# A decoder trunk on one core: nine instead of six blocks of each MLP's second product in the seven-product form

## The chip, the cores and the metric

The kernel runs on one core of a Trainium2 chip. The metric is the device time of one execution in microseconds; the time of a kernel is the median of several executions. Before the change this is 611.49 us (three executions, 611.18 to 611.83).

Of the core's engines five matter: TensorE (matrix products; PE in the profile, its weight loads PEld), VectorE (DVE), ScalarE (ACT), GpSimd (POOL) and SyncE (SP), whose queue issues the transfers of the weights.

## The reference

The program is a two-layer decoder trunk on 256 tokens of width 1024, in float32:

```python
def sqrelu_mlp(x, w1, w2):
    h = jax.nn.relu(x @ w1)
    return (h * h) @ w2

for layer in range(DEPTH):                       # DEPTH = 2
    hn = rms_norm(h, norm_gain[layer, 0])
    h = h + (stick_breaking_attention(hn, ...) if layer == 0 else nsa_attention(hn, ...))
    h = h + sqrelu_mlp(rms_norm(h, norm_gain[layer, 1]), mlp_w1[layer], mlp_w2[layer])
return rms_norm(h, final_norm)
```

w1 is 1024 x 4096 and w2 4096 x 1024. The change touches the two MLPs only.

## The kernel before

**Products of split numbers.** Each float32 operand a is split into a rounded part (h, cast to fp32r by ScalarE) and the rest (l = a - h, by VectorE). A product a b is then three matmuls: ah bh, ah bl, al bh (`mm3`, L209 to L211). In the first product of the MLP two of these go into one matmul 512 columns wide (L214, `wide`).

**Weights** come as tiles of 128 x 2048, one transfer each, in the order of use. `fetch` issues a transfer when one of three raw buffers is free; `split` (L121) makes the h and l tiles (wh, wl, three buffers each, shared by w1 and w2) in two steps of 1024 columns: a cast on ScalarE (L155), a subtraction on VectorE (L158). `step` calls it as work goes on, up to three tiles ahead.

**A block of the MLP.** The 4096 hidden columns are cut into 16 blocks c of 256. Tile wa[c] holds w1's columns of block c, wb[c] the two row blocks of w2 (each 128 x 1024). For each block the first product is made in two halves f = 0, 1 of 16 matmuls (`products`, L375) into a bank pu. `evac` (L384) copies the bank on ScalarE (mr) and adds its two parts on VectorE (mu, L390). After both halves `hidden` (L392) applies relu and the norm's scale (L396), squares (ScalarE, L398), and splits into hh and hl (L410, L411), with the sums that the second product needs (hx, L402 to L408).

**The second product** of a block is a 2 x 2 product: two hidden halves by two token tiles, against two row blocks of w2 and two column halves of 512. It takes eight products of 128 x 512 (`plain`), or, for blocks in FEWER, seven by Winograd's form (`fewer`), whose operands are sums of the hidden tiles and sums of w2's quarters. Each entry of the tables is (bank, hidden tile, which weights: 0 for w2's own split and 1 for the sums, first column). The first four entries run behind the next block's second half (part 0), the others in the middle of the block after that, between its two halves (part 1). The extra banks of the seven-product form are put together once by `fold`, behind block 12.

**The sums of w2.** For a block in FEWER `split` takes a branch (L135 to L149). It makes four sums of 512 columns (tx, 2048 wide, one buffer; L141, L143, L144), splits them into tp (one buffer, 2048 columns of h and of l), and splits the three quarters of w2 itself that are needed (1536 columns).

**The order.** TensorE's order is that of the code here (it is kept). A scheduler with its own costs places the instructions of the other engines, each of which runs its list in order.

Of the kernel before, what the change touches and what calls it, by code (L numbers as in the profile page):

```python
# [7 lines left out]
F32 = mybir.dt.float32  # L8
F32R = mybir.dt.float32r
# [5 lines left out]
P = 128  # L15
D = 1024
# [12 lines left out]
NEG = -1e30  # L29
GELU_C = 2.0 * 0.7978845608028654  # L30

FEWER = (2, 4, 6, 8, 10, 12)

C_ID, C_CA, C_CAP, C_ANY, C_COS, C_SIN, C_BLK, C_PW, C_END = (
    0, 128, 256, 640, 642, 674, 706, 710, 711)
# [29 lines left out]
def hybrid_kernel(ctx, tc, x, xca, xcb, eye, gcols, gfin, wqk, wva, wvb, wo0, wkv, wq, wg, rot, wo1, w1, w2, cw1, cw2, cpos, gate_b, cmask, consts, out):  # L65
    nc = tc.nc
# [8 lines left out]
    def f32(a):  # L75
        return a.bitcast(F32)
# [4 lines left out]
    def pair(shape, name):  # L81

        return cp.tile([P, 2, *shape], F32R, tag="x", name=name, bufs=2)

    def bank(name, dt=F32):
        return ps.tile([P, 512], dt, tag="a", name=name, bufs=4)
# [11 lines left out]
    made, raws = [], {}  # L98
# [3 lines left out]
    mixed = {}  # L102
# [18 lines left out]
    def split(pin=False):  # L121

        j, c = at
        src, n, plain = stream[j]
        if plain:

            made.append([wp.tile([P, n], F32, tag=f"w{a}", name="wc", bufs=3) for a in "hl"])
            for a in range(2):
                nc.sync.dma_start(made[j][a], src[a])
            at[:] = (j + 1, 0)  # L130
            return
        if c == 0:
            made.append((wp.tile([P, n], F32R, tag="wh", name="wh", bufs=3),
                         wp.tile([P, n], F32R, tag="wl", name="wl", bufs=3)))
        if j in mixed:  # L135
            h, lo = made[j]
            four = raws[j].rearrange("p (a q) -> p a q", q=512)
            tx, th, tl = mixed[j]()
            t4 = tx.rearrange("p (a q) -> p a q", q=512)
            if c == 0:  # L140
                nc.vector.tensor_sub(t4[:, 0:2, :], four[:, 1::2, :], four[:, 0:2, :])  # L141
            else:
                nc.vector.tensor_sub(t4[:, 2, :], four[:, 3, :], t4[:, 0, :])  # L143
                nc.vector.tensor_sub(t4[:, 3, :], four[:, 2, :], t4[:, 2, :])  # L144
            for dh, dl, src, r in ((h, lo, raws[j], slice(c, c + (1024 if c else 512))), (th, tl, tx, slice(c, c + 1024))):
                nc.scalar.copy(dh[:, r], src[:, r])  # L146
                nc.vector.tensor_sub(dl[:, r], src[:, r], f32(dh[:, r]))  # L147
            at[:] = (j, 1024) if c == 0 else (j + 1, 0)
            if c:  # L149
                fetch()  # L150
            return
        m = n // 4 if j < 2 else n // 2
        r = slice(c, c + m)
        h, lo = made[j]
        ins = nc.scalar.copy(h[:, r], raws[j][:, r])  # L155
        if pin:
            tc.keep_in_program_order(ins)
        nc.vector.tensor_sub(lo[:, r], raws[j][:, r], f32(h[:, r]))  # L158
        at[:] = (j, c + m) if c + m < n else (j + 1, 0)
        if c + m == n and j != NV - 1:  # L160
            fetch()
# [160 lines left out]
    def mlp(layer, gi, xt, mid, ap):  # L322

        wa, wb = i_m[layer]
        tp = pair([2048], "tp")
        tx = []

        def sums():
            if not tx:
                tx.append(ap.tile([P, 2048], F32, name="tx", bufs=1))  # L330
            return tx[0], tp[:, 0], tp[:, 1]

        for c in FEWER:
            mixed[wb[c]] = sums
        bank_of = {}
        last_few = FEWER[-1]

        plain = ((2, 1, 0, 0), (2, 3, 0, 1024), (4, 0, 0, 0), (4, 2, 0, 1024),
                 (5, 0, 0, 512), (5, 2, 0, 1536), (3, 4, 0, 512), (3, 5, 0, 1536))
        fewer = ((1, 1, 0, 0), (2, 3, 0, 1024), (3, 7, 0, 1536), (4, 2, 1, 1536),  # L340
                 (5, 4, 1, 0), (6, 5, 1, 1024), (7, 6, 1, 512))

        def product(m, a, kind, o, hT, c, q=slice(0, 512), o_bank=None, first=False):
            w = W(wb[c])
            if kind:
                w = sums()[1:]
            if o_bank is None:
                first = m not in bank_of
                if first:
                    bank_of[m] = bank(f"acc{m}") if 2 <= m <= 5 else zs[{1: 1, 6: 3, 7: 2}[m]]  # L350
                o_bank = bank_of[m]
            mm3(o_bank[:, q], (hT[0][:, a, :], hT[1][:, a, :]), cut(w, o + q.start, o + q.stop), first,
                c == NFC - 1 or c == last_few and m in (1, 6, 7))

        def second(c, hT, part):
            ps_ = fewer if c in FEWER else plain
            for i, e in enumerate(ps_[:4] if part == 0 else ps_[4:]):
# [26 lines left out]
        def evac(c, f, pu):  # L384
            if c not in parts:
                parts[c] = ap.tile([P, 2, 512], F32, name="mr", bufs=1), ap.tile([P, 512], F32, name="mu")
            r, u = parts[c]
            with tc.high_priority(offset=300):
                nc.scalar.copy(r[:, f, :], pu)  # L389
            nc.vector.tensor_add(u[:, f * 256:(f + 1) * 256], r[:, f, 0:256], r[:, f, 256:512])  # L390

        def hidden(c):  # L392
            r, u = parts.pop(c)
            few = c in FEWER
            uv = u.rearrange("p (f q) -> p f q", f=2)
# [60 lines left out]
        for c in range(3, NFC):  # L456
# [22 lines left out]
            h = hidden(c)  # L479
# [744 lines left out]
```

## Time and profile before

| | before |
|---|---|
| median of the runs | 611.49 us |
| span of the profiled execution | 609.3 us |
| TensorE busy | 598.4 us (98%) |
| VectorE busy | 503.4 us (83%) |
| ScalarE busy | 397.8 us (65%) |
| GpSimd busy | 61.2 us (10%) |
| mean granted TensorE clock | 0.997 |

The profiled execution is one of its own; its span runs from the first to the last instruction, and the runs' median, measured without a profile, lies 2.2 us above it.

The two MLPs lie at about 112 to 290 us and 425 to 596 us. In the profile, the chain of waits follows the work that ended last back from the end; "PE pu L214 x16" is one half of a block's first product. A timeline row gives start, length, engine, line, operation, output and inputs, and in brackets how long the engine was idle before and on whom it waited. A window's row gives each engine's busy time in a stretch, overlaps counted once.

### The profile page before, as it was taken

To read this page: it belongs to the slowest core of one execution; us is meant where nothing else is said; L and a number is where in the kernel's file an instruction comes from. 1 tells how busy PE (TensorE), PEld (TensorE's weight loads), DVE (VectorE), ACT (ScalarE), POOL (GpSimd) and SP (SyncE) were. 2 spreads that over 40 slices of the span, in tenths; PEclk is the share of its full clock that TensorE was granted. 3 is DMA by queue.
4 is the path that set the end of the run, shared out by engine and by line. 5 is a ranking of instruction groups with operands and counts; after the bars stand their busy time and mean duration, and the time that the engine had idled before them with its cause. 6 is when DMAs were issued, how large, how long until landed. Compare 5 with 4: busy or idle time off the path is not lost.

```text
span 609.3 us, 9115 instructions
## 1 busy us (share of the span) xinstructions
PE 598.4 (98%) x3449; PEld 501.0 (82%) x3449; DVE 503.4 (83%) x830; ACT 397.8 (65%) x658; POOL 61.2 (10%) x85
## 2 busy tenths in 40 slices
PE   9999999999999999999999989999999999999995
PEld 6888887888888888888998677677888888888884
DVE  5598996889998898887797799755799889889875
ACT  6677765786676666754842597854867657666651
POOL 0211010000000000000330265440000000000000
PEclk9999999999999999999999999999999999999998
DMA  8973331655554555364477721311457365546401
GB/s 316 358 266 138 139 139 70 232 183 201 214 208 156 189 210 213 134 248 162 162 260 290 247 120 70 105 70 58 166 192 276 113 233 208 186 160 219 195 2 69
DMA packets 18812, 109.35 MB, mean 179 GB/s; under 512 B 2512, under 2 KB 3792, under 8 KB 6736
## 3 DMA queue, kind: packets, MB, share of 16 engines
q1 hardware_dynamic: 17472, 107.06, 47.9%
q10 hardware_dynamic: 1296, 1.70, 0.8%
q8 instruction: 27, 0.44, 0.3%
q14 instruction: 17, 0.14, 0.1%
HBM read 106.66 MB, written 1.05 MB: 177 GB/s over the span
## 4 chain that ended last, share of the span: by engine, by line
PE 91%; DVE 3%; DMA 2%; issue 2%; ACT 1%; POOLq 0%; POOL 0%; DVEq 0%; ACTq 0%
PE pu L214 29%; PE acc L209 10%; PE acc L211 10%; PE acc L210 10%; PE qk L214 7%; PE po L214 3%; PE z L214 2%; PE pk L209 2%; PE pk L211 2%; PE pk L210 2%; DMA wc<-in_cw 2%; PE ptp L217 2%; PE pu L211 1%; PE pu L210 1%; PE pu L209 1%
## 5 line engine op out<-in xcount | busy, mean ns | idle before, releaser
L158 DVE TENSOR_TENSOR wl<-raw,wh 128x1024 fp32r<-128x1024 f32 (+1 forms) x168 | 199.7, 1210 | 43.2 <-ACT wh L155 39.6
L155 ACT CAST wh<-raw 128x1024 fp32r<-128x1024 f32 (+1 forms) x168 | 167.3, 1030 | 67.3 <-PE acc L211 28.4
L214 PE MATMUL pu<-xn,wh 128*128 128x512 f32 x512 | 131.5, 391 | 0.0
L214 PEld LDWEIGHTS pu<-xn,wh 128*128 128x128 f32 x512 | 95.1, 188 | 19.5 <-DVE xn L283 0.2
L214 PE MATMUL pu<-xn,wl 128*128 128x256 f32 x512 | 76.5, 282 | 0.0
L214 PEld LDWEIGHTS pu<-xn,wl 128*128 128x128 f32 x512 | 72.0, 190 | 5.1
L211 PE MATMUL acc<-wh,hl 128*128 128x512 f32 (+1 forms) x184 | 72.3, 393 | 0.0
L210 PE MATMUL acc<-wl,hh 128*128 128x512 f32 (+1 forms) x184 | 72.0, 391 | 0.0
L209 PE MATMUL acc<-wh,hh 128*128 128x512 f32 (+1 forms) x184 | 72.0, 391 | 0.0
L389 ACT COPY mr<-pu 128x512 f32<-128x512 f32 x64 | 37.2, 581 | 15.7 <-PE pu L214 15.7
L211 PEld LDWEIGHTS acc<-wh,hl 128*128 128x128 f32 x184 | 34.6, 188 | 8.0 <-DVE hl L411 0.3
L209 PEld LDWEIGHTS acc<-wh,hh 128*128 128x128 f32 x184 | 34.8, 189 | 6.7
L210 PEld LDWEIGHTS acc<-wl,hh 128*128 128x128 f32 x184 | 34.6, 188 | 6.8
L411 DVE TENSOR_TENSOR hl<-hx,hh 128x768 fp32r<-128x768 f32 (+1 forms) x32 | 32.1, 1004 | 6.9 <-ACT hh L410 6.9
L146 ACT CAST tp<-tx 128x1024 fp32r<-128x1024 f32 x24 | 25.2, 1049 | 18.9 <-DVE tx L141 17.7
L398 ACT ACTIVATE hx<-mu 128x512 f32<-128x512 f32 x32 | 20.2, 630 | 24.3 <-DVE mu L396 24.3
L410 ACT CAST hh<-hx 128x768 fp32r<-128x768 f32 (+1 forms) x32 | 28.1, 877 | 8.1 <-DVE hx L408 7.8
L214 PE MATMUL qk<-xa,wh 128*128 128x512 f32 x128 | 32.5, 394 | 0.0
L390 DVE TENSOR_TENSOR mu<-mr 128x256 f32<-128x256 f32 x64 | 26.8, 420 | 5.7 <-ACT mr L389 5.7
L988 ACT ACTIVATE pe<-pe,nm 128x256 f32<-128x256 f32 (+1 forms) x64 | 28.2, 442 | 4.4 <-DVE nm L986 3.3
L1002 POOL TENSOR_TENSOR pe<-pe,rs 128x512 f32<-128x512 f32 (+1 forms) x32 | 28.3, 917 | 25.7 <-DVE rs L997 16.5
L147 DVE TENSOR_TENSOR tp<-tx,tp 128x1024 fp32r<-128x1024 f32 x24 | 29.2, 1218 | 0.0
(231 smaller groups left out, 1114.0 us busy)
## 6 DMA issues: line engine op xcount, KB each, us to landing
raw<-in_w SPq DMA_DIRECT2D x64, 1024.0 KB, 4.8
raw<-in_wqk SPq DMA_DIRECT2D x8, 1024.0 KB, 5.2
raw<-in_wo SPq DMA_DIRECT2D x8, 1024.0 KB, 4.8
raw<-in_wkv SPq DMA_DIRECT2D x6, 1024.0 KB, 4.8
raw<-in_wq SPq DMA_DIRECT2D x4, 1024.0 KB, 4.9
wc<-in_cw SPq DMA_DIRECT2D x4, 1024.0 KB, 9.5
raw<-in_wvb SPq DMA_DIRECT2D x5, 512.0 KB, 7.4
raw<-in_wva SPq DMA_DIRECT2D x6, 256.0 KB, 4.3
```

Source lines behind the costliest of these rows:

```text
L147: nc.vector.tensor_sub(dl[:, r], src[:, r], f32(dh[:, r]))
L155: ins = nc.scalar.copy(h[:, r], raws[j][:, r])
L158: nc.vector.tensor_sub(lo[:, r], raws[j][:, r], f32(h[:, r]))
L209: pe(nc.tensor.matmul(o, a[0], b[0], start=first, stop=False, skip_group_check=True))
L210: pe(nc.tensor.matmul(o, a[0], b[1], start=False, stop=False, skip_group_check=True))
L211: pe(nc.tensor.matmul(o, a[1], b[0], start=False, stop=last, skip_group_check=True))
L214: pe(nc.tensor.matmul(o, a, b, start=first, stop=last, skip_group_check=True))
L389: nc.scalar.copy(r[:, f, :], pu)
L410: nc.scalar.copy(hh[:, r], hx[:, r])
L411: nc.vector.tensor_sub(hl[:, r], hx[:, r], f32(hh[:, r]))
L988: nc.scalar.activation(e, e, AF.Exp, scale=-1.0, bias=nm[:, hd, t, b:b + 1], accum_out=rs[:, hd, t, b:b + 1])
L1002: nc.gpsimd.tensor_tensor(sv, sv, rs[:, hd, t, :][:, :, None].to_broadcast([P, 2, n]), op=OP.mult)
```

## The change

Nine blocks of each MLP take the seven-product form instead of six, in rows of three with one plain block between (2, 3, 4, 6, 7, 8, 10, 11, 12).

Of the sums of w2 one, the second quarter less the first, is now made in place in the raw tile and split with w2's own quarters, so that all 2048 columns of the raw tile are split and 1536 of sums (tx). The tables change with it: the products of part 0 read w2's own split only, those of part 1 the sums only. There are two pairs of sum buffers (tp and tq), taken in turn.

In `evac` the two mu adds of 256 columns become one of 512 behind the second half. The scratch for dynamic transfers is set to 8192 bytes.

```diff
-FEWER = (2, 4, 6, 8, 10, 12)
+FEWER = (2, 3, 4, 6, 7, 8, 10, 11, 12)
...
         if j in mixed:
+            if c == 0:
+                mixed[j] = mixed[j]()
             h, lo = made[j]
-            four = raws[j].rearrange("p (a q) -> p a q", q=512)
-            tx, th, tl = mixed[j]()
-            t4 = tx.rearrange("p (a q) -> p a q", q=512)
+            tx, th, tl = mixed[j]
+            q = raws[j].rearrange("p (a q) -> p a q", q=512)
+            t = tx.rearrange("p (a q) -> p a q", q=512)
             if c == 0:
-                nc.vector.tensor_sub(t4[:, 0:2, :], four[:, 1::2, :], four[:, 0:2, :])
+                nc.vector.tensor_sub(t[:, 0, :], q[:, 3, :], q[:, 1, :])
+                nc.vector.tensor_sub(q[:, 1, :], q[:, 1, :], q[:, 0, :])
+                todo = ((h, lo, raws[j], slice(D, 2 * D)), (h, lo, raws[j], slice(0, D)))
             else:
-                nc.vector.tensor_sub(t4[:, 2, :], four[:, 3, :], t4[:, 0, :])
-                nc.vector.tensor_sub(t4[:, 3, :], four[:, 2, :], t4[:, 2, :])
-            for dh, dl, src, r in ((h, lo, raws[j], slice(c, c + (1024 if c else 512))), (th, tl, tx, slice(c, c + 1024))):
+                nc.vector.tensor_sub(t[:, 1, :], q[:, 3, :], q[:, 1, :])
+                nc.vector.tensor_sub(t[:, 2, :], q[:, 2, :], t[:, 1, :])
+                todo = ((th, tl, tx, slice(0, D)), (th, tl, tx, slice(D, 1536)))
+            for dh, dl, src, r in todo:
...
-        tp = pair([2048], "tp")
...
+        tps = [pair([1536], "tp"), ap.tile([P, 2, 1536], F32R, name="tq", bufs=1)]
+
+        for i, c in enumerate(FEWER):
+            mixed[wb[c]] = lambda tp=tps[i % 2]: (ap.tile([P, 1536], F32, name="tx", bufs=1), tp[:, 0], tp[:, 1])
...
-        fewer = ((1, 1, 0, 0), (2, 3, 0, 1024), (3, 7, 0, 1536), (4, 2, 1, 1536),
-                 (5, 4, 1, 0), (6, 5, 1, 1024), (7, 6, 1, 512))
+        fewer = ((1, 1, 0, 0), (2, 3, 0, 1024), (3, 7, 0, 1536), (5, 4, 0, 512),
+                 (4, 2, 1, 1024), (6, 5, 1, 512), (7, 6, 1, 0))
...
-            nc.vector.tensor_add(u[:, f * 256:(f + 1) * 256], r[:, f, 0:256], r[:, f, 256:512])
+            if f:
+                nc.vector.tensor_add(u.rearrange("p (f q) -> p f q", f=2), r[:, :, 0:256], r[:, :, 256:512])
...
-    nc = _bacc.Bacc("TRN2", target_bir_lowering=False, num_devices=1)
+    nc = _bacc.Bacc("TRN2", target_bir_lowering=False, num_devices=1, dynamic_dma_scratch_size=8192)
```

The diff adds lines in `split`, so the same code stands a few lines lower in the changed kernel between there and `mlp`: `mm3` is L214 to L216, `wide`'s matmul L219, the plain split L160 and L163, the split of the branch for FEWER L151 and L152, its sums L143, L144, L147 and L148.

**TensorE, block 12 of layer 0 (the end of part 0, the next first half, the begin of part 1).** Before (acc2 to acc5 and pu0, pu1 are banks, wh and wl weights, tp the sums):

```order
L209 MATMUL acc3_1391<-wh_2314,hh_2306 128x512
L210 MATMUL acc3_1391<-wl_2315,hh_2306 128x512
L211 MATMUL acc3_1391<-wh_2314,hl_2307 128x512
L209 MATMUL acc4_1377<-tp_1153,hh_2306 128x512
L210 MATMUL acc4_1377<-tp_1153,hh_2306 128x512
L211 MATMUL acc4_1377<-tp_1153,hl_2307 128x512
L214 MATMUL pu0_1311<-xn_932,wh_2361 128x512 x8
L214 MATMUL pu0_1311<-xn_932,wl_2362 128x256 x8
L209 MATMUL acc5_1384<-tp_1153,hh_2306 128x512
```

After:

```order
L214 MATMUL acc3_1389<-wh_2341,hh_2333 128x512
L215 MATMUL acc3_1389<-wl_2342,hh_2333 128x512
L216 MATMUL acc3_1389<-wh_2341,hl_2334 128x512
L214 MATMUL acc5_1382<-wh_2341,hh_2333 128x512
L215 MATMUL acc5_1382<-wl_2342,hh_2333 128x512
L216 MATMUL acc5_1382<-wh_2341,hl_2334 128x512
L219 MATMUL pu0_1310<-xn_932,wh_2386 128x512 x8
L219 MATMUL pu0_1310<-xn_932,wl_2387 128x256 x8
L214 MATMUL acc4_1375<-tp_1153,hh_2333 128x512
```

The fourth product of part 0 now reads w2's own split (wh, wl), and the sums are first read behind the next first half.

**VectorE, a seven-product block of layer 0.** Before, in the block that makes w2's tile 12 (raw is the loaded tile, mr and mu the hidden block's evacuation and sum):

```order
L147 TENSOR_TENSOR tp_1153<-tx_1432,tp_1153 128x1024
L147 TENSOR_TENSOR wl_2315<-raw_2206,wh_2314 128x512
L390 TENSOR_TENSOR mu_2249<-mr_2248 128x256
L147 TENSOR_TENSOR wl_2315<-raw_2206,wh_2314 128x1024
L396 SCALAR_TENSOR_TENSOR mu_2249<-mu_2249,rb_1220 128x512
L147 TENSOR_TENSOR tp_1153<-tx_1432,tp_1153 128x1024
L402 TENSOR_TENSOR hx_2304<-hx_2304 128x128
L403 TENSOR_TENSOR hx_2304<-hx_2304 128x128
L404 TENSOR_TENSOR hx_2304<-hx_2304 128x128
L405 TENSOR_TENSOR hx_2304<-hx_2304 128x128
L390 TENSOR_TENSOR mu_2338<-mr_2337 128x256
L411 TENSOR_TENSOR hl_2307<-hx_2304,hh_2306 128x896
```

After, in the middle block of the last three (hidden block 11, tile 11 of w2):

```order
L148 TENSOR_TENSOR tx_2249<-raw_2125,tx_2249 128x512
L405 TENSOR_TENSOR hx_2237<-hx_2237 128x128
L152 TENSOR_TENSOR tq_1154<-tx_2249,tq_1154 128x1024
L152 TENSOR_TENSOR tq_1154<-tx_2249,tq_1154 128x512
L411 TENSOR_TENSOR hl_2240<-hx_2237,hh_2239 128x896
L163 TENSOR_TENSOR wl_2293<-raw_2184,wh_2292 128x1024
```

and in the third (hidden block 12, tile 12):

```order
L152 TENSOR_TENSOR wl_2342<-raw_2222,wh_2341 128x1024
L148 TENSOR_TENSOR tx_2343<-raw_2222,tx_2343 128x512
L163 TENSOR_TENSOR wl_2387<-raw_2281,wh_2386 128x1024
L411 TENSOR_TENSOR hl_2334<-hx_2331,hh_2333 128x896
L152 TENSOR_TENSOR tp_1153<-tx_2343,tp_1153 128x1024
L152 TENSOR_TENSOR tp_1153<-tx_2343,tp_1153 128x512
L163 TENSOR_TENSOR wl_2387<-raw_2281,wh_2386 128x1024
```

Before, hl stood behind both splits of the sums and an add of the next block. Now it stands behind them in the middle block and ahead of them in the third, where one split of the next w1 tile (wl_2387) is also ahead of it.

**SP's queue in layer 1's attention.** Before:

```order
L113 DMA raw_3003<-in_wq 128x2048
L719 DMA kT_2663<-kT_2663 64x512
L720 DMA kT_2663<-kT_2663 64x512
L113 DMA raw_3050<-in_wq 128x2048
L129 DMA wc_3064<-in_cw1 128x2048
```

After:

```order
L113 DMA raw_3026<-in_wq 128x2048
L113 DMA raw_3073<-in_wq 128x2048
L719 DMA kT_2686<-kT_2686 64x512
L720 DMA kT_2686<-kT_2686 64x512
L129 DMA wc_3087<-in_cw1 128x2048
```

One load of w_q moved ahead of an exchange of key halves (kT); the loads of the compression weights (wc) stand behind both as before. Outside the MLPs nothing else changes its place on SP, and nothing on GpSimd.

More of the change, by code (lines that the diff above doesn't have):

```diff
@@ L324, in mlp @@
         wa, wb = i_m[layer]
-        tp = pair([2048], "tp")
[L326 to L334, printed above, removed]
+        tps = [pair([1536], "tp"), ap.tile([P, 2, 1536], F32R, name="tq", bufs=1)]
+        for i, c in enumerate(FEWER):
+            mixed[wb[c]] = lambda tp=tps[i % 2]: (ap.tile([P, 1536], F32, name="tx", bufs=1), tp[:, 0], tp[:, 1])
         bank_of = {}
@@ L345, in product @@
             if kind:
-                w = sums()[1:]
+                w = mixed[wb[c]][1:]
             if o_bank is None:
```

## The prediction

> **What bounds the kernel now.** I read the page first (busy shares, granted clock, the chain's shares), then the chain of waits in order of time, then one window in the MLP and the timelines of VectorE and ScalarE in it.
>
> ```profile
> PE 598.4 (98%) x3449; PEld 501.0 (82%) x3449; DVE 503.4 (83%) x830; ACT 397.8 (65%) x658; POOL 61.2 (10%) x85
> ...
> PEclk9999999999999999999999999999999999999998
> ...
> PE 91%; DVE 3%; DMA 2%; issue 2%; ACT 1%; POOLq 0%; POOL 0%; DVEq 0%; ACTq 0%
> ```
>
> TensorE is busy for 98% at full clock and is 91% of the chain. The chain inside MLP 0, where each "x16" row is one half of a block's first product:
>
> ```profile
> 183.99 2.77 PE pu L214 x16
> ...
> 189.53 2.77 PE pu L214 x16
> ...
> 195.07 2.77 PE pu L214 x16
> ...
> 199.93 2.77 PE pu L214 x16
> ...
> 205.47 2.77 PE pu L214 x16
> ```
>
> The halves start 5.54 us apart, and 4.86 us where the products between them belong to a seven-product block (195.07 to 199.93). So a block takes 2 x 5.54 = 11.08 us, one whose second half is short 4.86 + 5.54 = 10.40 us, and TensorE never pauses. Removing a product here shortens the run, provided that its operands stay on time. VectorE makes them, and one plain with one seven-product block show how busy it is:
>
> ```profile
> core 0: us, PE busy (x) PEld busy (x) DVE busy (x) ACT busy (x) POOL busy (x), PEclk, DMA share, GB/s
> ...
> 184.00:205.47 21.47, 21.47 (x110) 18.27 (x110) 19.27 (x27) 14.25 (x18) 0.00 (x0) 1.00 0.52 196
> ```
>
> VectorE has 2.2 us to spare in 21.47, ScalarE 7.2. This pair mixes a heavy and a light block, and the change alters the mixture. So the price of each VectorE instruction is needed, from its timeline in that window (start, length, line, operation, tile):
>
> ```profile
> 186.03 0.29 DVE L402 TENSOR_TENSOR hx<-hx 128x128 f32<-128x128 f32 x1
> 186.23 0.28 DVE L403 TENSOR_TENSOR hx<-hx 128x128 f32<-128x128 f32 x1
> 186.43 0.28 DVE L404 TENSOR_TENSOR hx<-hx 128x128 f32<-128x128 f32 x1
> 186.75 0.29 DVE L405 TENSOR_TENSOR hx<-hx 128x128 f32<-128x128 f32 x1
> ...
> 188.31 1.09 DVE L411 TENSOR_TENSOR hl<-hx,hh 128x896 fp32r<-128x896 f32 x1 [0.41 <-ACT hh L410]
> 190.66 3.50 DVE L158 TENSOR_TENSOR wl<-raw,wh 128x1024 fp32r<-128x1024 f32 x3 [1.26 <-ACT wh L155]
> 194.07 0.42 DVE L390 TENSOR_TENSOR mu<-mr 128x256 f32<-128x256 f32 x1
> 194.41 1.22 DVE L158 TENSOR_TENSOR wl<-raw,wh 128x1024 fp32r<-128x1024 f32 x1
> 195.54 0.69 DVE L396 SCALAR_TENSOR_TENSOR mu<-mu,rb 128x512 f32<-128x512 f32 x1
> 196.15 1.22 DVE L158 TENSOR_TENSOR wl<-raw,wh 128x1024 fp32r<-128x1024 f32 x1
> 197.28 0.42 DVE L408 TENSOR_TENSOR hx<-hx 128x256 f32<-128x256 f32 x1
> 197.62 1.22 DVE L158 TENSOR_TENSOR wl<-raw,wh 128x1024 fp32r<-128x1024 f32 x1
> 198.75 0.95 DVE L411 TENSOR_TENSOR hl<-hx,hh 128x768 fp32r<-128x768 f32 x1
> 199.62 0.42 DVE L390 TENSOR_TENSOR mu<-mr 128x256 f32<-128x256 f32 x1
> 199.96 1.22 DVE L141 TENSOR_TENSOR tx<-raw 128x1024 f32<-128x1024 f32 x1
> 201.21 0.69 DVE L143 TENSOR_TENSOR tx<-raw,tx 128x512 f32<-128x512 f32 x1
> 201.93 0.69 DVE L144 TENSOR_TENSOR tx<-raw,tx 128x512 f32<-128x512 f32 x1
> 202.54 1.22 DVE L147 TENSOR_TENSOR tp<-tx,tp 128x1024 fp32r<-128x1024 f32 x1
> 203.68 0.69 DVE L147 TENSOR_TENSOR wl<-raw,wh 128x512 fp32r<-128x512 f32 x1
> 204.30 0.43 DVE L390 TENSOR_TENSOR mu<-mr 128x256 f32<-128x256 f32 x1
> ```
>
> What an instruction costs is the distance to the next start, about 0.08 less than its length, since the records overlap: 1024 columns 1.14 us ((3.50 - 1.22) / 2), 512 columns 0.61 or, where the next one needs its result, 0.72 (201.21 to 201.93), 256 columns 0.34, the four 128-column sums 0.93, hl 0.87 or 1.01.
>
> A plain block today: four splits 4.56, two mu adds 0.68, L396 0.61, hx 0.34, hl 0.87: 7.06 us. A seven-product block: w1 split 2.28, weight sums 1.25 + 0.72 + 0.61 = 2.58, their and w2's splits 3 x 1.14 + 0.62 = 4.04, mu 0.68, L396 0.61, hx 0.93, hl 1.01: 12.13 us. Together 19.2, the window's 19.27. So a seven-product block costs VectorE 12.1 us against TensorE's 10.40, and only the plain block behind it (7.1 against 11.08) pays that back.
>
> The window's 27 instructions have lengths of 22.2 us in sum, more than the 21.47 us they stand in with idle time besides: lengths don't add up here. [...]
>
> **The change, part by part.**
>
> *Three more seven-product blocks per layer.* Each drops one product of three 512-column matmuls: 5.54 - 4.86 = 0.68 us, six in both layers, **-4.1 us**.
>
> *VectorE's work.* The sums are four of 512 columns (2.44 to 2.88 us by the 0.61 and 0.72 above) for 2.58; the in-place one makes up for the fourth buffer column, and the split columns stay 2048 + 1536. One 512-column mu add (0.61) replaces two (0.68). So 11.9 to 12.4 us a block; I take 12.1, as in the printed order other work stands between most dependent sums. A plain block falls to 7.0. Three in a row are 36.3 us against 31.2 of TensorE: VectorE falls 1.7 us behind per block, 5.1 per trio, and wins 4.1 back in the plain one, 1.0 short per group of four. Over blocks 2 to 12 it needs 9 x 12.1 + 2 x 7.0 = 122.9 us, TensorE 9 x 10.40 + 2 x 11.08 = 115.8, and 117.8 today. If VectorE's lag reached TensorE in full, the layer would be slower by 5. So the question is how far it may lag.
>
> *The cover.* The tightest chain through VectorE is the hidden one: pu is copied (mr), added (mu), squared, summed (hx), cast (hh), split (hl), and the third matmul of the next block's last quarter reads hl. In the window hl of the seven-product block ends at 188.31 + 1.09 = 189.40; the half that starts at 189.53 ends at 192.30, two matmuls of 0.23 follow, so 192.76 is its due time: slack 3.4 us. A second such block in a row arrives 1.7 later (slack 1.7), a third 3.4 later (0.0), and each finished group of four adds 1.0. The printed order gives something back: in the third block hl stands ahead of both tp splits, 1.14 + 0.62 = 1.76, in the middle one behind them. That leaves 1.7 and 1.8 in the first trio, 0.7 and 0.8 in the second, -0.3 and -0.2 in the third. The first trio's 1.7 a block also fits behind the weight loads:
>
> ```profile
> 186.85 0.59 ACT L389 COPY mr<-pu 128x512 f32<-128x512 f32 x1 [1.21 <-PE pu L214]
> 187.33 0.94 ACT L410 CAST hh<-hx 128x896 fp32r<-128x896 f32 x1
> 189.57 2.96 ACT L155 CAST wh<-raw 128x1024 fp32r<-128x1024 f32 x3 [1.29 <-PE acc L211]
> ```
>
> The cast of w1 waited 1.29 us for TensorE to free w2's buffers, and both w1 splits ended at 190.66 + 1.14 + 1.22 = 193.0, 2.1 us before their half at 195.07. In the changed kernel the second part of a seven-product block reads sums alone, so w2's own buffers come free one half earlier (2.77 us and three products, 4.9 us), and the sums' splits, 1.76 us a block, fall due a half later than w2's (5.5 us); the second pair of sum buffers lets them be written meanwhile. This cover is new, and VectorE's lag can sit in it.
>
> *What it costs all the same.* Below: nothing, if the order always lets hl and mr pass. Above: if hl kept its place behind the sums in every block, the third block is short by 1.0 in the second trio; paid there, the lag goes back and the third trio is short by 1.0 again, so 2.0 a layer, 4 in all. The printed order is nearer to the lower end; with 0.3 us short in one trio and something for ten or so waits per block I take 0.5 us a layer, **+1.0 us**.
>
> *The single mu add* now waits for both halves. The first half's mr copy of the next block stands behind it through ScalarE's square; the bank it empties is the one the second half writes (L214 pu0 both times), so a late add stops TensorE there after 2.1 us. ScalarE has 7 us idle per pair, one cast (0.95) and the copy (0.6) fit into 2.1: zero, as long as VectorE's lag stays below about 4.
>
> *The queues and the scratch size.* SP issues one w_q load ahead of two key exchanges instead of behind them; the loads of cw1 stay behind all three. TensorE's whole wait for those is 0.6 us, so this is worth between -0.6 and +0.6; I take zero. [...]
>
> ```profile
> L214 PE MATMUL ph<-wc,bt 128*64 128x256 f32 x64 | 7.6, 384 | 0.6 <-DMA wc<-in_cw 0.6
> ...
> q1 hardware_dynamic: 17472, 107.06, 47.9%
> q10 hardware_dynamic: 1296, 1.70, 0.8%
> q8 instruction: 27, 0.44, 0.3%
> q14 instruction: 17, 0.14, 0.1%
> ```
>
> **Sum.** -4.1 + 1.0 = -3.1 us. The profiled span of 609.3 becomes 606.2; the median of the runs lies 2.2 us above that span, so **608.4 us**.
>
> **The rivals.**
>
> *VectorE decides (slower).* If the cover were only today's 3.4 us, since mu, hx and hl stand in one in-order queue with everything else, each trio would stop TensorE for 5.1 - 3.4 = 1.7 us (a plain block wins back all that is left): six trios 10.2, less 4.1, **617.6 us**. For it: 19.27 of 21.47 busy already, and a surplus of 7.1 us a layer. Against it: the earlier buffers and the later due time of the sums. It decides once the cover per trio is below 5.1 - 4.1 / 6 = 4.4 us; at 2.1 us (today's slack of w1) it would be 18 - 4.1 = 14 us slower.
>
> *Lengths add up (slower, far).* If VectorE's instructions could not overlap once it is full, a seven-product block would take 13.2 us (the lengths above) and a plain one 7.6: 8.3 us lag per trio, 3.5 won back, against a cover of 3.4 + 1.76 = 5.2. Stops of 3.1, 4.8 and 4.8 us a layer: 25.4 - 4.1 = 21 us slower, **632.8 us**. The overlap in every row above speaks against it. [...]
>
> *The gain is given back (no change).* The upper end above, 4 us of stops, cancels 4.1: **611.4 us**. For it: slacks of 0.7 us and less in the second and third trio, within the error of my prices (0.1 us on ten instructions is 1 us). Against it: the order moves hl forward where it is tightest.
>
> *It does less than it says.* If the removed matmuls were not on the path, nothing would move. The 4.86 against 5.54 us in one trace, both without a pause, speak against it.
>
> **How the numbers follow.** The forecast, a cost of 0 to 2.5 us beside -4.1, has 0.60 (607.0 to 609.9); given back 0.17; VectorE decides 0.19; lengths add up 0.01; a better result than -4.1, through the SP order, 0.03. The range of 607.0 to 613.0 holds the forecast and the given-back case; the forecast's own is 607.0 to 609.9. Of this kernel about 0.2%, 1.2 us, can be told from no change: faster 0.63, same 0.17, slower 0.20.
>
> **What would show it.** TensorE: 18 matmuls fewer (three per new block), halves 4.86 and 5.54 apart in blocks 4 to 14; a longer distance is a stop, and its releaser says whether hl, mr or wl was late. VectorE: 12.1 us per seven-product block, over 95% busy in the trios, and the 1.3 us that ScalarE waits for w2's buffers gone there. I am wrong in size if new waits of TensorE on VectorE sum to over 2.5 us, in sign if over 4.1; wrong in the price if a block costs VectorE over 12.4.

## The result and the profile after

| | before | after |
|---|---|---|
| median of the runs | 611.49 us | 607.12 us (606.40 to 607.86) |
| ratio | 1 | 0.9928 (95% interval 0.9916 to 0.9941) |
| span of the profiled execution | 609.3 us | 605.3 us |
| VectorE busy | 503.4 us (83%) | 525.7 us (87%) |

The change makes the kernel 4.4 us faster; the forecast was 3.1 us. From the page of the changed kernel: busy times, granted clock by slices, and the chain's shares.

```profile
PE 594.5 (98%) x3431; PEld 497.9 (82%) x3431; DVE 525.7 (87%) x864; ACT 406.3 (67%) x670; POOL 61.3 (10%) x85
...
PEclk9999999999999999999999999999999999999999
...
PE 79%; DVE 14%; issue 3%; ACT 2%; DMA 1%; POOLq 0%; POOL 0%; DVEq 0%; ACTq 0%; SPq 0%
```

TensorE issues 18 matmuls fewer (3449 to 3431) at full clock (0.998 in the mean). New is VectorE's 14% of the chain, against 3%: in part of the run the chain now goes through it. Where TensorE sets the pace, the chain in order of time (start, length, what; MLP 1 of the changed kernel, with the first and the last row of its block loop) shows the halves:

```profile
454.48 5.56 PE pu L219 x32
...
505.07 2.77 PE pu L219 x16
...
509.91 2.77 PE pu L219 x16
...
515.45 2.77 PE pu L219 x16
...
520.31 2.77 PE pu L219 x16
...
525.85 2.77 PE pu L219 x16
...
530.69 2.77 PE pu L219 x16
...
536.23 2.77 PE pu L219 x16
...
541.77 2.77 PE pu L219 x16
...
578.49 5.56 PE pu L219 x32
```

505.07 to 536.23 is a row of three: distances of 4.84 to 4.86 and 5.54 us in turn, three times, with no stop. Then two distances of 5.54 for the plain block, to 541.77 and 547.31. The same two end rows in the chain of the kernel before:

```profile
456.39 5.56 PE pu L214 x32
...
582.53 5.56 PE pu L214 x32
```

From one to the other it took 126.14 us before and 124.01 now: -2.13 in layer 1, for nine matmuls of 0.231 us (2.08). What VectorE does meanwhile, by windows of layer 0 in the changed kernel (the whole stretch, then the time in which TensorE runs its second row of three):

```profile
core 0: us, PE busy (x) PEld busy (x) DVE busy (x) ACT busy (x) POOL busy (x), PEclk, DMA share, GB/s
143.00:257.40 114.40, 114.40 (x585) 97.53 (x584) 114.06 (x159) 82.60 (x105) 0.00 (x0) 1.00 0.54 193
194.39:225.56 31.17, 31.17 (x161) 26.59 (x160) 31.07 (x44) 22.05 (x29) 0.00 (x0) 1.00 0.62 235
```

and the first of these windows in the kernel before:

```profile
143.00:257.40 114.40, 114.40 (x585) 97.49 (x584) 101.58 (x137) 76.37 (x97) 0.00 (x0) 1.00 0.53 193
```

VectorE goes from 89% to 99.7% busy (114.06 of 114.40), and TensorE still does not stop in that stretch. How near it comes is read from hl and its reader, the third matmul of part 0. The least slack in the rows of three lies in block 11, by the timelines of VectorE and of TensorE:

```profile
243.16 1.09 DVE L411 TENSOR_TENSOR hl<-hx,hh 128x896 fp32r<-128x896 f32 x1
```

```profile
244.82 0.39 PE L216 MATMUL pu<-wh,hl 128*128 128x512 f32 x1
```

244.82 - (243.16 + 1.09) = 0.57 us. In the rows of three the slack so read is 1.1 and 2.1 in blocks 3 and 4, 2.1, 2.5 and 1.8 in blocks 6 to 8, 1.8, 0.6 and 1.0 in blocks 10 to 12. Read in the same way it was 3.2 before (block 6: 192.60 - 189.40, where the prediction has 3.4), and in the rows it never falls to zero.

The one stop that TensorE has in MLP 0 comes later, in the last block (15). TensorE's waits between 140 and 290 us (total, number, longest):

```profile
PE acc L214 <- ACT hh L410: 0.5, 1, 0.5
```

The timelines of VectorE and ScalarE say why:

```profile
278.21 2.35 DVE L163 TENSOR_TENSOR wl<-raw,wh 128x1024 fp32r<-128x1024 f32 x2
280.48 0.42 DVE L408 TENSOR_TENSOR hx<-hx 128x256 f32<-128x256 f32 x1
```

```profile
280.93 0.83 ACT L410 CAST hh<-hx 128x768 fp32r<-128x768 f32 x1 [1.91 <-DVE hx L408]
```

VectorE's list puts two weight splits of 1024 columns ahead of the short sum that ScalarE has waited 1.91 us for, and TensorE waits for ScalarE's cast. From 198 to 281 us the chain runs mostly over VectorE (with one weight transfer of 6.96 us at 252.14 in it): its 14%.

One wait is gone, by the groups of TensorE (busy us, mean ns, idle time before):

```profile
L219 PE MATMUL ph<-wc,bt 128*64 128x256 f32 x64 | 7.3, 382 | 0.0
```

These 64 matmuls stood 0.6 us for the loads of cw1 before. That the new order on SP did this is not shown: of the five traces with the old order on SP (the kernel before, nine blocks with the old buffers, one more VectorE instruction, and two executions of the kernel with two mu adds, all below) three have no such wait either, and the two executions of one kernel have 0 and 1.2 us. None of the nine traces with the new order has it.

The spans add up: layer 1 -2.13; layer 0 and the attention behind it -2.19 (310.42 us between the first rows of the two MLPs' block loops, 144.06 to 454.48, for 312.61 before, 143.78 to 456.39), which is -2.08 of matmuls and, as listed, -0.59 of that wait and +0.49 of the stop; +0.28 ahead of MLP 0; together -4.0, which is 609.3 - 605.3.

### The profile page after: what moved, and what is told of

It is laid out like the page before. It is cut to its first block, busy times and chain, and to the rows that moved or that the text cites. A ratio compares the mean times of both kernels' runs of the same rounds, so it can differ in the third digit from the quotient of the medians.

```text
span 605.3 us, 9135 instructions
## 1 busy us (share of the span) xinstructions
PE 594.5 (98%) x3431; PEld 497.9 (82%) x3431; DVE 525.7 (87%) x864; ACT 406.3 (67%) x670; POOL 61.3 (10%) x85
## 4 chain that ended last, share of the span: by engine, by line
PE 79%; DVE 14%; issue 3%; ACT 2%; DMA 1%; POOLq 0%; POOL 0%; DVEq 0%; ACTq 0%; SPq 0%
PE pu L219 22%; PE acc L214 7%; PE qk L219 7%; PE acc L216 7%; PE acc L215 7%; DVE wl L163 4%; PE po L219 3%; PE z L219 2%; PE pk L214 2%; PE pk L215 2%; PE pk L216 2%; PE ptp L222 2%; PE pu L216 1%; PE pu L215 1%; PE pu L214 1%
## 5 line engine op out<-in xcount | busy, mean ns | idle before, releaser
L163 DVE TENSOR_TENSOR wl<-raw,wh 128x1024 fp32r<-128x1024 f32 (+1 forms) x156 | 185.9, 1209 | 28.5 <-ACT wh L160 25.5
L160 ACT CAST wh<-raw 128x1024 fp32r<-128x1024 f32 (+1 forms) x156 | 156.2, 1028 | 59.7 <-DMA raw<-in_w 11.8
L219 PE MATMUL pu<-xn,wh 128*128 128x512 f32 x512 | 131.6, 391 | 0.0
L219 PEld LDWEIGHTS pu<-xn,wh 128*128 128x128 f32 x512 | 95.0, 188 | 19.6 <-DVE xn L288 0.2
L219 PE MATMUL pu<-xn,wl 128*128 128x256 f32 x512 | 76.5, 282 | 0.0
L219 PEld LDWEIGHTS pu<-xn,wl 128*128 128x128 f32 x512 | 72.1, 190 | 5.1
L214 PE MATMUL acc<-wh,hh 128*128 128x512 f32 (+1 forms) x166 | 65.0, 392 | 0.5 <-ACT hh L410 0.5
L216 PE MATMUL acc<-wh,hl 128*128 128x512 f32 (+1 forms) x166 | 65.1, 393 | 0.0
L215 PE MATMUL acc<-wl,hh 128*128 128x512 f32 (+1 forms) x166 | 64.9, 391 | 0.0
L151 ACT CAST wh<-raw 128x1024 fp32r<-128x1024 f32 x36 | 37.5, 1052 | 29.7 <-PE pu L219 17.7
L152 DVE TENSOR_TENSOR wl<-raw,wh 128x1024 fp32r<-128x1024 f32 x36 | 43.8, 1220 | 0.3
L214 PEld LDWEIGHTS acc<-wh,hh 128*128 128x128 f32 x166 | 31.4, 189 | 7.3 <-ACT hh L410 0.9
L216 PEld LDWEIGHTS acc<-wh,hl 128*128 128x128 f32 x166 | 31.2, 188 | 7.4 <-DVE hl L411 0.5
L411 DVE TENSOR_TENSOR hl<-hx,hh 128x896 fp32r<-128x896 f32 (+1 forms) x32 | 32.9, 1029 | 3.7 <-ACT hh L410 3.6
L410 ACT CAST hh<-hx 128x896 fp32r<-128x896 f32 (+1 forms) x32 | 28.7, 898 | 9.0 <-DVE hx L405 5.5
L219 PE MATMUL qk<-xa,wh 128*128 128x512 f32 x128 | 32.5, 394 | 0.0
L1002 POOL TENSOR_TENSOR pe<-pe,rs 128x512 f32<-128x512 f32 (+1 forms) x32 | 28.3, 917 | 25.7 <-DVE rs L997 16.5
L219 PEld LDWEIGHTS qk<-xa,wh 128*128 128x128 f32 x128 | 22.9, 189 | 4.3 <-issue 0.2
```

The costliest lines, as they stand in the source:

```text
L214: pe(nc.tensor.matmul(o, a[0], b[0], start=first, stop=False, skip_group_check=True))
L215: pe(nc.tensor.matmul(o, a[0], b[1], start=False, stop=False, skip_group_check=True))
L216: pe(nc.tensor.matmul(o, a[1], b[0], start=False, stop=last, skip_group_check=True))
L219: pe(nc.tensor.matmul(o, a, b, start=first, stop=last, skip_group_check=True))
L410: nc.scalar.copy(hh[:, r], hx[:, r])
L411: nc.vector.tensor_sub(hl[:, r], hx[:, r], f32(hh[:, r]))
```

## The experiments

All are compared with the kernel before on the same chip. Unless said otherwise, the edit is to the changed kernel. The scheduler places the other engines' lists anew for each version, so an experiment changes more than its edit shows: VectorE's order differs in each of them. What such an order is worth by itself was not measured.

**The changed tables with the old six blocks.**

```diff
-FEWER = (2, 3, 4, 6, 7, 8, 10, 11, 12)
+FEWER = (2, 4, 6, 8, 10, 12)
```

> The changed kernel with the old six seven-product blocks (2, 4, 6, 8, 10, 12): new sums, new tables, two sum buffers, one mu add, but the old number of matmuls. Theory (the gain is the 18 removed matmuls alone, the rest only keeps their operands on time): no change, 611.4 us (610.9 to 612.0); VectorE busy about 19.1 us in a pair of blocks as before. Rival (the new form of a block is itself cheaper for the path): 609 to 610 us.

Measured: 611.2 us, ratio 1.0000 (0.9991 to 1.0009). In the same window as above:

```profile
143.00:257.40 114.40, 114.40 (x585) 97.55 (x584) 101.71 (x132) 77.22 (x98) 0.00 (x0) 1.00 0.53 193
```

VectorE needs 101.71 us for 101.58 before. Tables, in-place sum, single add, order and scratch size together are worth nothing within 0.55 us; the gain is that of the three blocks more. The wait for cw1 is 0.0 here too and the span 608.5, 0.8 below that of before, which the runs' median does not follow. So the 0.6 us are not confirmed in times.

This version also answers a point of the prediction. ScalarE's waits for TensorE to free w2's buffers, between 143 and 260 us, before, with six blocks, and in the changed kernel:

```profile
ACT wh L155 <- PE acc L211: 11.3, 10, 3.0
```

```profile
ACT wh L160 <- PE acc L216: 9.1, 10, 1.2
```

```profile
ACT wh L160 <- PE acc L216: 1.8, 3, 1.2
```

The new tables alone leave most of these waits; with the rows of three they go, and ScalarE waits for w1's buffers instead (8.8 us in six waits). By the tables a seven-product block frees w2's own buffers at the end of part 0, a plain one in part 1, and the rows have fewer plain blocks. That ScalarE, behind a late VectorE, also comes later to these casts is not ruled out.

**Nine blocks with the old buffers and tables.** The edit is to the kernel before:

```diff
-FEWER = (2, 4, 6, 8, 10, 12)
+FEWER = (2, 3, 4, 6, 7, 8, 10, 11, 12)
```

Here part 1 of a block and part 0 of the next share the one pair of sum buffers, and in a row of three the program writes the next block's sums before part 1 has read this block's. So part 1 is computed with the wrong sums.

> The kernel before with nine blocks in FEWER and nothing else: one sum buffer of 2048 columns, old tables, two mu adds. Same matmuls as the changed kernel. Theory (cover): with one buffer the sums of the next block can't be split before the middle of the block after next, and w2's own buffers come free a half later, so VectorE's lag of 1.7 us a block reaches TensorE in every row of three: 613 to 622 us. Rival (VectorE was never near the path, the rework is dressing): 607.3 us.

Measured: 616.09 us, ratio 1.0076 (1.0061 to 1.0091). TensorE's waits:

```profile
PE pu L210 <- DVE tp L147: 5.4, 6, 2.0
```

That part 1 waits for the next block's sums is due to the sharing and not to a short cover, so this kernel does not separate the theories as I had meant. It shows two other things. The second pair of buffers is needed for the result itself. And a stop can cost more than its length, by windows around the longest one:

```profile
156.00:158.00 2.00, 0.02 (x1) 0.00 (x0) 2.00 (x5) 0.94 (x1) 0.00 (x0) 1.00 0.75 311
159.43:162.84 3.41, 3.41 (x10) 2.63 (x9) 3.23 (x4) 0.00 (x0) 0.00 (x0) 0.50 0.51 125
```

1.4 us behind a stop of 2.0 us the granted clock falls to 0.50, stays there for 3.41 us and is 1.00 again between 164 and 166 us: by estimate 3.41 / 2 = 1.7 us lost beside the stop. Not every stop of about that length does this. In layer 1 of the same trace one of 1.91 us is followed by full clock:

```profile
473.71 0.50 PE L210 MATMUL pu<-tp,hh 128*128 128x512 f32 x1 [1.91 <-DVE tp L147]
```

```profile
473.71:480.54 6.83, 6.83 (x33) 5.74 (x34) 6.61 (x8) 3.44 (x5) 0.00 (x0) 1.00 0.58 197
```

What decides whether the clock falls, no run here shows.

**One pair of sum buffers, otherwise the change.** The same part of the computation is wrong as above.

```diff
-            mixed[wb[c]] = lambda tp=tps[i % 2]: (ap.tile([P, 1536], F32, name="tx", bufs=1), tp[:, 0], tp[:, 1])
+            mixed[wb[c]] = lambda tp=tps[0]: (ap.tile([P, 1536], F32, name="tx", bufs=1), tp[:, 0], tp[:, 1])
```

> The changed kernel with one pair of sum buffers in use (tp for all nine blocks, tq unused). Theory: the splits of the sums of the next block wait until part 1 of the block before has read them, 4 to 5 us later than with two; VectorE's in-order list stands behind them, TensorE stops: 609 to 616 us. Rival (the new tables alone are enough, since the sums are due late): 607.1 us.

Measured: 635.63 us, ratio 1.0397 (1.0379 to 1.0415).

```profile
PE acc L214 <- ACT tp L151: 11.7, 6, 2.1
PE acc L215 <- DVE tp L152: 5.7, 10, 0.8
```

17.4 us of stops, the longest 2.1 us, and the granted clock falls to 0.50 again (between 216 and 220 us). They are again waits of part 1 for the next block's sums. How much time the second pair covers, with the right sums read, stays open: one pair cannot hold both.

**The fourth product of part 0 on the sums again.** The change had put w2's own product there.

```diff
-        fewer = ((1, 1, 0, 0), (2, 3, 0, 1024), (3, 7, 0, 1536), (5, 4, 0, 512),
-                 (4, 2, 1, 1024), (6, 5, 1, 512), (7, 6, 1, 0))
+        fewer = ((1, 1, 0, 0), (2, 3, 0, 1024), (3, 7, 0, 1536), (4, 2, 1, 1024),
+                 (5, 4, 0, 512), (6, 5, 1, 512), (7, 6, 1, 0))
```

> The changed kernel with two entries of the table exchanged: the product with a sum of w2 (4, 2, 1, 1024) goes into part 0, the one with w2's own split (5, 4, 0, 512) into part 1, as in the kernel before. w2's buffers come free 4.9 us later, one sum is due 3.5 us earlier; same products. Theory (cover from the tables): TensorE stops 0.5 to 2 us in each row of three, 609 to 615 us. Rival (two buffers alone are enough): 607.1 us.

Measured: 610.11 us, ratio 0.9981 (0.9972 to 0.9991), so 3.0 us of the 4.4 are lost. This exchange does two things: one sum falls due 3.5 us earlier (a half and a product), and w2's own buffers come free 3.5 us later (and not 4.9, as I had expected: their last reader is now the first product of part 1). The first shows in TensorE's waits:

```profile
PE acc L215 <- DVE tp L152: 1.0, 2, 0.5
```

**w2's own product late, no sum early.** To part the two, part 0 has three products, all of w2's own, and part 1 four:

```diff
-            for i, e in enumerate(ps_[:4] if part == 0 else ps_[4:]):
+            n0 = 3 if c in FEWER else 4
+            for i, e in enumerate(ps_[:n0] if part == 0 else ps_[n0:]):
```

> The changed kernel with three products in part 0 and four in part 1 of a seven-product block: the fourth product with w2's own split moves behind the next first half, ahead of the sums. w2's buffers come free one product into part 1 (3.5 us later than in the changed kernel), the sums are due 0.7 us later; same products. It takes apart what the exchange of two table entries (610.1 us) joined. If the due time of the sums was what cost there: 607.1 us (606.5 to 607.9). If the release of w2's buffers was: 609 to 611 us.

Measured: 608.76 us, ratio 0.9960 (0.9946 to 0.9975), 1.6 us above the change. The wait on the sums is gone and another stands in its place:

```profile
PE pu L215 <- DVE wl L152: 1.2, 2, 0.6
```

It is one on w2's own split, which the late release of its buffers explains. So the late release alone costs 1.6 us here, and neither theory holds alone: by subtraction the early due time would be worth the other 1.4. The trace of the exchange itself divides the loss otherwise. By the starts of its matmuls, the hold-ups there on sums take about 2.1 us over both layers and those on w2's own split (block 8, 213.03 us in layer 0, too short for the list of waits) about 0.8. Both act; their shares stay open.

**One more VectorE instruction per block.** A sum of 512 columns is made twice in each seven-product block, 0.6 us:

```diff
                 nc.vector.tensor_sub(t[:, 1, :], q[:, 3, :], q[:, 1, :])
+                nc.vector.tensor_sub(t[:, 1, :], q[:, 3, :], q[:, 1, :])
```

> The changed kernel with one sum of 512 columns made twice in each seven-product block (0.6 us of VectorE more per block, 5.5 us per layer, the result the same). Theory (the cover is nearly used up: in the trace of the changed kernel the least slack of hl is 0.6 us): VectorE's 5.5 us a layer reach TensorE but for 1 to 2 us: 613 to 616 us. Rival (cover left over): 607.1 to 608 us.

Measured: 614.92 us, ratio 1.0058 (1.0043 to 1.0073), 7.8 us above the change for 18 instructions that sum to 10.8, and within the 613 to 616 of the theory. TensorE's waits, and the timeline rows around one:

```profile
PE pu L217 <- DVE hl L412: 3.5, 4, 0.9
...
PE acc L217 <- DVE hl L412: 0.6, 2, 0.3
...
PE pu L220 <- DVE wl L164: 0.6, 2, 0.3
```

```profile
527.03 0.39 PE L216 MATMUL pu<-wl,hh 128*128 128x512 f32 x1
528.32 0.51 PE L217 MATMUL pu<-wh,hl 128*128 128x512 f32 x1 [0.90 <-DVE hl L412]
528.66 0.39 PE L215 MATMUL acc<-wh,hh 128*128 128x512 f32 x1
```

The instruction named most is the one that the prediction took for the tightest, hl. The waits sum to 4.7 only; most of the rest lies in TensorE's busy time (597.4 for 594.5 us, with as many matmuls). The rows show how. Matmuls of 0.39 us start 0.23 apart, one over the other; the one that waited starts 1.29 behind its predecessor and the next 0.34 behind that, so a wait listed as 0.90 costs 1.06 + 0.11 = 1.17 us. This kernel gives an estimate of the cover: at 11.70 + 0.60 = 12.3 us a block (the 11.70 follows below) VectorE falls behind by 9 x (12.3 - 10.40) = 17.1 us a layer and wins 2 x 4.1 back, 8.9 at the end of the third row of three. 3.9 a layer were lost, so VectorE may be about **5.0 us** late before TensorE stops. The count is not exact: the first row of three, 5.7 us late by it, passes without a stop. And hl has another place here (in block 11 of layer 0 it stands ahead of both splits of the sums, in the changed kernel behind them), so the added 0.6 us and the new order are not told apart.

**All eleven blocks 2 to 12.** No plain block is left between.

```diff
-FEWER = (2, 3, 4, 6, 7, 8, 10, 11, 12)
+FEWER = (2, 3, 4, 5, 6, 7, 8, 9, 10, 11, 12)
```

> The changed kernel with all eleven blocks 2 to 12 in the seven-product form, no plain block between. TensorE has 12 matmuls fewer than in the changed kernel (-2.8 us). Theory: VectorE needs 4 to 5 us more in each of the four added blocks and nowhere wins back; with the cover used up, 9 us a layer of stops: 618 to 627 us. Rival (each seven-product block gains 0.7 us): 604.3 us.

Measured: 621.79 us, ratio 1.0172 (1.0157 to 1.0187). With four products fewer than the change it is 14.7 us slower, within the 618 to 627 of the theory. TensorE's waits and one window:

```profile
PE pu L216 <- DVE hl L411: 7.2, 15, 0.5
PE pu L215 <- DVE wl L152: 2.9, 12, 0.3
```

```profile
532.88:544.58 11.70, 10.98 (x53) 8.85 (x53) 11.70 (x18) 7.99 (x12) 0.00 (x0) 1.00 0.48 179
```

VectorE is busy for 11.70 of 11.70 us and sets the pace, at 17 instructions a block (the window's 18 have the hl of two blocks). So this kernel gives the price of a seven-product block directly, from hl to hl in VectorE's timeline, with some of the parts (a cost is the distance to the next start):

```profile
528.56 0.68 DVE L144 TENSOR_TENSOR raw<-raw 128x512 f32<-128x512 f32 x1
529.16 0.28 DVE L405 TENSOR_TENSOR hx<-hx 128x128 f32<-128x128 f32 x1
529.37 0.68 DVE L147 TENSOR_TENSOR tx<-raw 128x512 f32<-128x512 f32 x1
529.97 1.22 DVE L163 TENSOR_TENSOR wl<-raw,wh 128x1024 fp32r<-128x1024 f32 x1
...
532.24 1.08 DVE L411 TENSOR_TENSOR hl<-hx,hh 128x896 fp32r<-128x896 f32 x1
533.24 0.68 DVE L148 TENSOR_TENSOR tx<-raw,tx 128x512 f32<-128x512 f32 x1
...
543.94 1.09 DVE L411 TENSOR_TENSOR hl<-hx,hh 128x896 fp32r<-128x896 f32 x1
```

532.24 to 543.94 is **11.70 us**: four sums at 0.60 (2.4), four splits of 1024 columns at 1.13 to 1.14 (4.55), the split of 1536 columns of sums in two (1.74), the mu add and L396 at 0.60 each, four hx sums at 0.20 (0.8), hl 1.00. Where a sum stood right behind the one whose result it needs, the distance was 0.72 before; here other work stands between, and it is 0.60. By it, and again as an estimate, eleven blocks leave VectorE 11 x 1.3 = 14.3 us late a layer; less the 5.0 of cover that is 9.3, for two layers 18.6, less four products (2.8): 15.8 us slower than the change. The measured 14.7 makes the cover 5.5 us.

**The two mu adds of the kernel before,** in the changed kernel:

```diff
-            if f:
-                nc.vector.tensor_add(u.rearrange("p (f q) -> p f q", f=2), r[:, :, 0:256], r[:, :, 256:512])
+            nc.vector.tensor_add(u[:, f * 256:(f + 1) * 256], r[:, f, 0:256], r[:, f, 256:512])
```

> The changed kernel with the two mu adds of 256 columns of the kernel before. VectorE 0.07 us more per block, 1.1 us per layer, but the first half's add no longer waits for the second half. Theory (only VectorE's time counts): 607.1 to 609 us. Rival (the late add cost something through mr): 606.0 to 606.8 us.

Measured: 608.24 us, ratio 0.9952 (0.9936 to 0.9969), but the runs spread from 606.25 to 608.72, and the profiled execution, with a span of 604.5, has no stop in an MLP at all. It was measured once more.

> The version with two mu adds once more, with more rounds, since its first runs lay between 606.3 and 608.7 us. In its trace TensorE has no stop in the MLP, in that of the changed kernel one of 0.5 us (hh of block 15 late). Theory (0.07 us of VectorE per block more, VectorE with next to no slack in rows of three): 607.1 to 608.5 us. Rival (the earlier add takes the stop away and costs nothing): 606.0 to 606.9 us.

Measured: 606.69 us, ratio 0.9925 (0.9913 to 0.9937), which can't be told from the 0.9928 of the change. The same kernel thus gave 608.24 and 606.69 us, on either side of the 607.12 of the change. The single add neither helps nor hurts within some 1 us, though it saves VectorE 0.07 us a block: inconclusive below that. Its two traces also differ by 1.2 us in the wait for cw1. The 0.5 us stop at the end of MLP 0 is in neither, which suggests that it hangs on the order there.

**Sums on GpSimd.** VectorE is full in the rows of three (31.07 us busy of 31.17 in the second) and GpSimd idle there (0.00); four sums off VectorE would take 2.4 us from each block. Three versions: all four sums in the nine blocks, the same in eleven blocks, and only the two sums of the second step in eleven blocks.

```diff
-                nc.vector.tensor_sub(t[:, 0, :], q[:, 3, :], q[:, 1, :])
-                nc.vector.tensor_sub(q[:, 1, :], q[:, 1, :], q[:, 0, :])
+                nc.gpsimd.tensor_sub(t[:, 0, :], q[:, 3, :], q[:, 1, :])
+                nc.gpsimd.tensor_sub(q[:, 1, :], q[:, 1, :], q[:, 0, :])
...
-                nc.vector.tensor_sub(t[:, 1, :], q[:, 3, :], q[:, 1, :])
-                nc.vector.tensor_sub(t[:, 2, :], q[:, 2, :], t[:, 1, :])
+                nc.gpsimd.tensor_sub(t[:, 1, :], q[:, 3, :], q[:, 1, :])
+                nc.gpsimd.tensor_sub(t[:, 2, :], q[:, 2, :], t[:, 1, :])
```

> The changed kernel with the four sums of w2 of each seven-product block made by GpSimd, which does nothing in the MLP before (1.1 us for 512 columns by its rows of the kernel before, 4.4 us per block). VectorE loses 2.4 us a block. Theory (TensorE never waits for VectorE in the changed kernel, so relief is worth nothing by itself): 606.8 to 607.6 us. Rival 1 (TensorE still loses time to VectorE in places that the waits do not show): 605 to 606.5 us. Rival 2 (the two engines slow each other on the same tiles): 608 us or more, with VectorE's 1024-column split over 1.22 us.

> The same with all eleven blocks 2 to 12. Theory (VectorE's 11.7 us a block, seen in the run with eleven blocks, was all that stood in the way): VectorE 9.3 us a block against 10.40 of TensorE, no stops, four blocks more at -0.68 us: 604.3 us (603.8 to 605.5). Rival (slower engines on shared tiles, or GpSimd's sums late for the splits): 608 us or more.

> All eleven blocks, GpSimd makes only the two sums of the second step, VectorE those of the first. VectorE 10.5 us a block against 10.40. Theory: 1 us a layer short less the cover of some us: 604.3 to 606 us. Rival (slower engines on shared tiles): 608 us or more, less than the version with all four sums on GpSimd.

Measured: 673.23 us (ratio 1.1023, 1.1004 to 1.1041), 688.57 (1.1271, 1.1254 to 1.1288) and 653.71 (1.0699, 1.0673 to 1.0724): the rival of slower engines holds in all three. The groups of the first version between 143 and 300 us, of GpSimd and of VectorE (busy us, mean ns), and TensorE's largest wait in the whole execution:

```profile
L143 POOL TENSOR_TENSOR tx<-raw 128x512 f32<-128x512 f32 x8 | 15.1, 1884 | 79.1 <-DMA raw<-in_w 75.3 <-DVE tp L152 3.8
```

```profile
L405 DVE TENSOR_TENSOR hx<-hx 128x128 f32<-128x128 f32 x9 | 6.7, 741 | 0.1
```

```profile
PE pu L219 <- ACT mr L388: 22.7, 12, 2.9
```

The same VectorE group in the changed kernel:

```profile
L405 DVE TENSOR_TENSOR hx<-hx 128x128 f32<-128x128 f32 x18 | 5.1, 286 | 0.0
```

and one subtraction of the first version during which VectorE had nothing to do:

```profile
202.36 1.29 POOL L147 TENSOR_TENSOR tx<-raw 128x512 f32<-128x512 f32 x1
```

In the first version instructions of both engines take longer: VectorE's short sum L405 goes from 286 to 741 ns in the mean, L396 from 0.69 to 1.02 us, and GpSimd's subtractions take up to 1.88 us in the mean instead of 1.29. The expected 1.1 us was too low even without VectorE beside it (1.29): the attention's L1002, from which it came (1.10 us), multiplies a tile by one number per row and is no such subtraction. That these longer instructions alone make the 66 us (673.23 for 607.12) was not shown: GpSimd's sums take longer than VectorE's even alone (1.29 us for 0.69), and TensorE's stops come with lowered clocks (0.95 in the mean between 143 and 300 us).

No version is faster than the change; the one with two adds is its equal.

## Why the prediction was right, and where it was not

The sign, the mechanism and the time hold: 607.12 us against 608.4, within the range. That the time came so near is in part luck, by the third and the fourth point below.

- *The matmuls, -4.1.* Right: 18 fewer, 4.84 to 4.86 us beside 5.54 in every new block, -4.2 over both layers by the halves, and no gain without them (six blocks: 1.0000).
- *The price of a seven-product block, 12.1.* Too high: 11.70 measured. The sums cost 2.4 and not 2.58, the hx sums 0.8 and not 0.93 (in the one block that I read, L405 stood right behind the sum whose result it needs and started 0.32 us after it, for 0.20 between the others; here a sum of w2 stands between). At 11.70 VectorE falls 1.3 us behind per block, 3.9 per row of three, and the plain block wins back 4.1: the 1.0 that each group of four was to carry on does not exist.
- *The stops, +1.0.* **This is the mis-sized term.** Measured: 0 in the rows of three, 0.5 as listed in all, and that at the end of MLP 0, a place I had not looked at, where VectorE's list has two splits ahead of a short sum. The 1.0 was a choice between bounds of 0 and 4, so that 0.5 lies near it is luck. The slacks expected for hl (1.7, 0.7 and -0.3 in the three rows) were really 1.1 to 2.1, 1.8 to 2.5 and 0.6 to 1.8. They do not shrink from row to row as expected, are least in the third row, and stay above zero.
- *The cover, 5.2 in the rival's sum, with 4.4 as the point from which VectorE decides.* Near in size: 5.0 to 5.5 by the estimates from the two kernels that overran it. 3.9 stays below, 8.9 does not. One of its reasons was misread: that part 1 of a seven-product block reads sums alone is not new (before, block 12's part 1 begins with acc5 on tp too), so w2's buffers came free no later there. The 1.29 us that ScalarE waited were for a plain block's part 1, and such waits go with the rows of three and not with the tables (11.3 us before, 9.1 with the new tables and six blocks, 1.8 with nine). What the order of the products protects is still real: holding w2's own buffers into part 1 cost 1.6 us, and this with an early sum 3.0. What the second pair of buffers covers by itself was not measured.
- *Single mu add, tables: 0.* Right within 0.55 us as a whole (six blocks, with the scratch size among the rest), and the add by itself within about 1 us. What the scratch size is worth by itself no run shows.
- *The order of SP, 0 with bounds of 0.6.* Within the bounds. The wait for cw1 (0.6) is gone in the trace, but it comes and goes with the old order too, and with six blocks the runs do not show a gain.
- *Sum.* -4.2 + 0.5 - 0.6 + 0.3 ahead of MLP 0 = -4.0 by the traces, as the spans differ; the runs differ by 4.4.

Of the rivals, "VectorE decides" fell for this kernel, but by little: 0.6 us more per block make it slower than before, and eleven blocks make it decide altogether. "Given back" asked for 4 us of stops, and 0.5 are there. "Lengths add up" is refuted by the eleven blocks: 11.70 us for instructions whose lengths sum to 13.1. "Does less than it says" falls with the halves.

## What to carry to other kernels

An engine that feeds the bound one in bursts may be over its budget for a while. What counts is the sum of its surplus over a run of heavy blocks against the time that its results may be late, and whether the light block behind wins all of it back; a busy share of 99.7% alone says neither yes nor no. To price such a block, make that engine the bound for one run and read the period: reading one block of an engine that still has idle time gave 12.1 for 11.70, and from this came the stops that were forecast and did not come. Part of the cover comes from which products run first, since these decide when operands fall due and when buffers come free: exchanging two products cost 3.0 of the 4.4 us.

## What the hardware showed that was not expected

- TensorE's granted clock fell to 0.50 for 3.41 us behind a stop of 2.04 us, by estimate 1.7 us lost beside the stop itself, and did not fall behind one of 1.91 us. In the kernel with one more VectorE instruction per block a stop at a granted clock of 1.00 cost more than its listed length too: 1.17 us for 0.90.
- VectorE was 99.7% busy over 114 us while the engine that it feeds had no stop.
- Subtractions on GpSimd beside VectorE went with longer instructions on both: up to 1.88 us in the mean for 1.29 alone there, 741 ns for 286 on VectorE.
